# Attention biases that come finished by transfer, and low weight parts from an accumulating transfer

## The chip, the cores and the metric

The kernel runs on one core of a Trainium2 chip. The metric is the device time of one execution in microseconds (us); before the change it is 1277.18 us, the median of 3 runs (1276.97 to 1279.51).

The core's engines are named as the profile names them: PE is TensorE (matrix products), DVE is VectorE, ACT is ScalarE, POOL is GpSimd, and SP is the engine whose queue issues most transfers. Each engine works through its own list of instructions in order, and waits for the others at semaphores. Transfers that SP or GpSimd issue run beside them on the DMA engines.

## The reference

Two residual layers of width 1024 over 512 tokens. The first mixes by a gated unit (gMLP), the second by an attention with a forget gate (FoX), and each is followed by a channel MLP with a squared ReLU. All inputs are 32-bit floats. The change touches the attention alone:

```python
def fox_mixer(h, w_in, b_f, q_g, k_g, w_out):
    p = h @ w_in
    q, k, v, gate, f_logit = jnp.split(p, [W, 2 * W, 3 * W, 4 * W], axis=-1)
    ...
    log_f = jax.nn.log_sigmoid((f_logit + b_f).astype(jnp.float32))
    c = jnp.cumsum(log_f, axis=1).transpose(0, 2, 1)
    for i in range(S // Q_BLOCK):
        ...
        logits = jnp.einsum('bhtd,bhsd->bhts', qb, kb).astype(jnp.float32) * scale
        logits = logits + c[:, :, q0:kend, None] - c[:, :, None, :kend]
        logits = jnp.where(t_idx >= s_idx, logits, -jnp.inf)
        probs = jax.nn.softmax(logits, axis=-1).astype(vb.dtype)
        outs.append(jnp.einsum('bhts,bhsd->bhtd', probs, vb))
    ...
    o = o * jax.nn.sigmoid(gate)
    return o @ w_out
```

There are 16 heads of width 64; `c` is the running sum of the log forget gates, and the bias of a query t on a key s is `c[t] - c[s]`. Rows are worked in 4 blocks of 128 queries, and block i sees the first (i + 1) x 128 keys.

## The kernel before

**Products in three parts.** PE multiplies numbers of a shorter format (fp32r). So each 32-bit factor is cut in a high part, which is its copy in that format, and a low part, which is what the copy lacks; a product is high x high + high x low + low x high (`mm3`, whose matmuls the profile shows at L243). For weights this is done by the class `Stream`. It cuts all weights into chunks of up to 128 x 1024 numbers and for each chunk does three things in order: `_load` (L80) fetches it from HBM into one of 3 buffers `raw` through SP's queue; ACT copies it into the high part `wh` (L85); and another engine subtracts, `wl = raw - wh` (L86). There are 4 buffers each for `wh` and `wl`. `take` hands a chunk to the products and at that moment starts the cut of the third chunk after it, and the load of the third after that.

**Who subtracts.** For most chunks L86 runs on DVE. The 52 chunks of the attention (20 of 768 columns, 16 of 1024, 12 of 512 and 4 of 800) are in the range `ws.pooled`, and there it runs on POOL.

**The attention stage.** It takes the stretch from about 610 to 925 us. The weights of a pair of heads are projected (`project`, matmuls `pq`), and beside them, one matmul group at a time, run the attention steps of the pair before (`attend`): norms of q and k (L722 to L726, of which L725 is a power on POOL and L726 the scaling of `y` on DVE), turns by PE (`tq`, `tk`), logits (`lg`), softmax, turns of the probabilities (`tp`, copied to high and low parts `pth` and `ptl` at L842 and L843), products with the values (`ot`), and the output gate. The gates (`pg`) and the output projection (`po`) are further work between them. The order of PE's instructions in this stage is fixed in the program; a scheduler places the instructions of the other engines and of SP around it.

**The bias.** Once, `forget` works out `c` for all heads: `ct` holds -c with a token per partition, `cs` holds c with a head per row, and SP writes `cs` to a scratch tensor `cd` in HBM (L652). Then, for each head, SP fetches its row of `cd` into all 128 partitions (`cb`, L785, two buffers), and for each block i POOL adds the block's own column of `ct` (L792, tile `bias{i}`, one buffer for each i) and sets the entries of later keys in the diagonal square to a large number (L794). Since the sign of the logits is turned, DVE adds bias and logits and takes the least of each row in one instruction (L803); ACT takes the exponential and its row sums (L804); DVE takes the reciprocal (L806) and scales the four blocks (L808).

**The order around the change.** POOL's list in this stage holds L86, L792, L794, L725 and a few sums of squares of the norms at its ends; DVE's list holds all of the softmax besides the exponential; SP's list holds the loads of the chunks and the fetches of `cb`, and a transfer there that waits for its buffer holds back what is queued behind it.

Of the kernel before, what the change touches and what calls it, by code (L numbers as in the profile page):

```python
# [8 lines left out]
F32 = mybir.dt.float32  # L9
F32R = mybir.dt.float32r  # L10
AF = mybir.ActivationFunctionType
ALU = mybir.AluOpType
# [4 lines left out]
P = 128  # L17
D = 1024
S = 512
KB = D // P  # L20
NT = S // P
E = 2 * D
FF = 4 * D
H = 16
# [30 lines left out]
class Stream:  # L55
# [27 lines left out]

    def _parts(self, hi, lo, t, eng):
        self.nc.scalar.activation(hi, t, AF.Copy)  # L85
        eng.tensor_tensor(lo, t, hi.bitcast(F32), op=ALU.subtract)  # L86

    def _split(self):
        nc, i = self.nc, self.split
        kind = self.chunks[i][1]  # L90
        t, n = self.raw[i] if kind == "first" else self.raw.pop(i)
        hi = self.pool.tile([P, CHUNK_COLS], F32R, tag="wh", name=f"wh{i}", bufs=self.bufs[1])
        lo = self.pool.tile([P, CHUNK_COLS], F32R, tag="wl", name=f"wl{i}", bufs=self.bufs[1])
        eng = nc.gpsimd if i in self.pooled else nc.vector
        pieces = [slice(n // 2, n)] if kind == "second" else self._pieces(i, n)
        for sl in pieces:
            self._parts(hi[:, sl], lo[:, sl], t[:, sl], eng)
        self.parts[i] = (hi, lo)
        if kind == "second":
            self._sums(i, self.raw.pop(i - 1)[0], t)  # L100
        self.split += 1

    def _sums(self, i, f, g):
        nc, sp = self.nc, self.sums_pool
# [9 lines left out]
        for q, s in enumerate((s12, s43)):  # L114
            hi = sp.tile([P, 2, h], F32R, tag="sh", name=f"sh{i}_{q}", bufs=2)
            lo = sp.tile([P, 2, h], F32R, tag="sl", name=f"sl{i}_{q}", bufs=2)
            self._parts(hi, lo, s, nc.vector)
            made += [(hi[:, e], lo[:, e]) for e in range(2)]
# [20 lines left out]
def trunk(ctx: ExitStack, tc: tile.TileContext, A, out, stages=4):  # L139
    nc = tc.nc  # L140
    pe, dve, act, pool = nc.tensor, nc.vector, nc.scalar, nc.gpsimd
# [6 lines left out]
    dram = ctx.enter_context(tc.tile_pool(name="dram", bufs=1, space=DRAM))  # L148
# [15 lines left out]
    chunks = []  # L164
# [21 lines left out]
    chunks += mlp_chunks(A["m0_1"], A["m0_2"])  # L186
    lo_pool = [len(chunks)]
    if stages > 2:
        for kind, n in FOX_ORDER:
# [8 lines left out]
            elif kind == "w":  # L198
                chunks += [A["fw_o"][n, m] for m in range(2)]
    lo_pool.append(len(chunks))  # L200
    if stages > 3:
        chunks += mlp_chunks(A["m1_1"], A["m1_2"])
    ws = Stream(nc, wp, chunks, bufs=(3, 4), ahead=3, load_ahead=3, halved=(0, 1))
    ws.pooled = range(*lo_pool)

# [142 lines left out]
    with ExitStack() as st:  # L348
# [6 lines left out]
        for g in range(4):  # L355
            pv = [(psB if g == 1 and i < 3 else psA)(f"pv{g}_{i}") for i in range(NT)]
            for c in range(4):
                wh, wl = (t.rearrange("p (k n) -> p k n", k=2) for t in ws.take())
                for i in range(NT):
                    for kk in range(2):  # L360
                        k = 2 * c + kk
                        sl = slice(i * P, (i + 1) * P)
# [243 lines left out]
    with ExitStack() as st:  # L606
        fs = st.enter_context(tc.tile_pool(name="fs", bufs=2))
        fp = st.enter_context(tc.tile_pool(name="fp", bufs=2))
# [13 lines left out]
        ct = fp.tile([P, NT, H], F32, tag="ct", name="ct", bufs=1)  # L622
        cd = dram.tile([H, S], F32, tag="cd", name="cd")

        def forget(pq):

            fl = fp.tile([P, NT, H], F32, tag="fl", name="fl", bufs=1)
# [23 lines left out]
            act.activation(cs, pt[:H], AF.Copy, scale=-1.0)  # L651
            nc.sync.dma_start(cd, cs)  # L652
            did.add("F")
# [104 lines left out]
        def attend(p, y):  # L758
# [21 lines left out]
            for e in range(2):  # L780
                hd = 2 * p + e
                yield lag, ("T", p - 1, e) if p else "F"
                lag = 0.0
                cb = fp.tile([P, S], F32, tag="cb", name=f"cb{hd}")
                nc.sync.dma_start(cb, cd[hd].partition_broadcast(P))  # L785
                ees = []
                sm = fs.tile([P, NT], F32, tag="sm", name=f"sm{hd}")
                mn = fs.tile([P, NT], F32, tag="mn", name=f"mn{hd}")
                for i in range(NT):
                    n = (i + 1) * P  # L790
                    bi = fp.tile([P, n], F32, tag=f"bias{i}", name=f"bias{hd}_{i}", bufs=1)
                    pool.tensor_scalar(bi, cb[:, :n], 1.0, ct[:, i, hd : hd + 1], op0=ALU.mult, op1=ALU.add)  # L792
                    dg = bi[:, i * P :]
# [182 lines left out]
```

## Time and profile before

| | us |
|---|---|
| median of 3 runs | 1277.18 |
| the profiled execution | 1277.01 |
| its span in the profile | 1275.3 |

A time is that of a whole execution; the span is the part of it between the first and the last instruction in the profile, here 1.7 us less. The page of the profile gives, for each engine, the busy time, its share of the span and the number of instructions; the number after an x is always a count. A row of a group names the line of the kernel, the engine, the operation, what it writes and reads, the shapes and the count, then the busy time and the mean length of one in ns, and last the idle time of the engine ahead of it and what ended it. A row of waits names who waited, for whom, the sum in us, how often, and the longest. In a table of windows a row begins with its start and end and its length in us; then come the busy times of PE, PEld (the loading of PE's weights), DVE, ACT and POOL with the number of instructions, the granted clock of PE, and the share of time that the DMA engines worked, with GB/s. Busy time of a group is a union, so that neighbours which overlap by some 0.07 us make it a little less than count x mean.

### The profile page before, as it was taken

Reading aid. Unit: us, or ns where it says so; the run is one execution under the profiler, and the core shown is the slowest. Engines: PE = TensorE matmul, PEld = TensorE weight load, DVE = VectorE, ACT = ScalarE, POOL = GpSimd, SP = SyncE. Lnnn points to the kernel's source line nnn. Section 1 sums busy time; section 2 is a strip of 40 time slices with the busy share of each in tenths; the row PEclk is TensorE's granted clock in tenths of the full one; section 3 lists DMA queues with packets and bytes.
Section 4 is the critical chain, followed back from the end, with each engine's and each line's share of the span. In section 5 each row is a group of like instructions: output and inputs, shape, how many; then the busy total and the mean of one; then the engine's idle time right before and its main releaser. Section 6 shows DMA issues by size and latency. Waiting matters only on the chain.

```text
span 1275.3 us, 18354 instructions
## 1 busy us (share of the span) xinstructions
PE 1262.1 (99%) x7108; PEld 1114.0 (87%) x7108; DVE 877.2 (69%) x1206; ACT 624.9 (49%) x981; POOL 484.7 (38%) x415
## 2 busy tenths in 40 slices
PE   9999999999999999999999999999999999999998
PEld 7888888888999999998899899898888999999987
DVE  7347767677867676765537777777887767676763
ACT  7334423246534344443467687678465444444430
POOL 4108433025423232310657667667173322323200
PEclk9999999999999999999999999999999999999999
DMA  7333233233233332323223222223223323232321
GB/s 250 97 107 92 83 91 91 84 98 93 90 116 100 100 102 97 111 89 96 80 81 103 84 82 76 84 77 106 83 67 116 116 84 116 84 116 83 118 81 66
DMA packets 39607, 124.01 MB, mean 97 GB/s; under 512 B 4816, under 2 KB 5840, under 8 KB 39520
## 3 DMA queue, kind: packets, MB, share of 16 engines
q1 hardware_dynamic: 39232, 122.82, 30.4%
q8 instruction: 56, 0.92, 0.3%
q14 instruction: 31, 0.25, 0.1%
q10 hardware_dynamic: 288, 0.02, 0.0%
HBM read 120.69 MB, written 2.13 MB: 96 GB/s over the span
## 4 chain that ended last, share of the span: by engine, by line
PE 89%; DVE 6%; ACT 2%; issue 1%; POOL 1%; DMA 1%; DVEq 0%; ACTq 0%; POOLq 0%
PE po L243 36%; PE da L243 11%; PE bc L243 9%; PE pq L243 8%; PE pv L243 8%; PE pu L243 7%; PE ph L243 3%; PE pg L243 2%; PE ot L243 2%; DVE xl L271 1%; PE lg L243 1%; PE tp L248 1%; PE sp L426 1%; DVE ee L808 1%; DVE y L726 1%
## 5 line engine op out<-in xcount | busy, mean ns | idle before, releaser
L85 ACT ACTIVATE wh<-raw 128x1024 fp32r<-128x1024 f32 (+3 forms) x230 | 219.7, 957 | 270.9 <-PE po L243 83.5
L86 DVE TENSOR_TENSOR wl<-raw,wh 128x1024 fp32r<-128x1024 f32 (+1 forms) x178 | 252.5, 1432 | 46.2 <-ACT wh L85 45.4
L243 PE MATMUL po<-zl,wh 128*128 128x512 f32 x512 | 200.6, 392 | 1.3 <-DVE zl L500 1.3
L243 PE MATMUL po<-zh,wh 128*128 128x512 f32 x512 | 199.9, 391 | 0.0
L243 PE MATMUL po<-zh,wl 128*128 128x512 f32 x512 | 199.5, 390 | 0.0
L556 DVE TENSOR_TENSOR x<-x,po 128x512 f32<-128x512 f32 x128 | 87.2, 683 | 106.1 <-PE po L243 106.1
L86 POOL TENSOR_TENSOR wl<-raw,wh 128x768 fp32r<-128x768 f32 (+3 forms) x52 | 102.4, 1969 | 125.7 <-ACT wh L85 123.2
L110 POOL TENSOR_TENSOR ssum<-raw 128x512 f32<-128x512 f32 x26 | 35.5, 1364 | 268.6 <-DMA raw<-in_m_dram 256.8
L85 ACT ACTIVATE sh<-ssum 128x1024 fp32r<-128x1024 f32 x52 | 55.2, 1061 | 164.5 <-POOL ssum L111 95.8
L243 PEld LDWEIGHTS po<-zh,wl 128*128 128x128 f32 x512 | 96.2, 188 | 19.5
L243 PEld LDWEIGHTS po<-zh,wh 128*128 128x128 f32 x512 | 96.5, 188 | 17.9
L243 PEld LDWEIGHTS po<-zl,wh 128*128 128x128 f32 x512 | 96.6, 189 | 17.8 <-DVE zl L500 1.6
L243 PE MATMUL pq<-wh,xh 128*128 128x384 f32 (+2 forms) x256 | 88.4, 345 | 0.0
L410 POOL TENSOR_SCALAR vn<-v,mv,lnr 128x128 f32<-128x128 f32 x64 | 63.1, 999 | 59.5 <-DVE vl L414 59.4
L243 PE MATMUL pq<-wh,xl 128*128 128x384 f32 (+2 forms) x256 | 83.1, 325 | 0.0
L243 PE MATMUL pq<-wl,xh 128*128 128x384 f32 (+2 forms) x256 | 82.7, 323 | 0.0
L86 DVE TENSOR_TENSOR sl<-ssum,sh 128x1024 fp32r<-128x1024 f32 x52 | 65.9, 1268 | 18.2 <-ACT sh L85 18.1
L112 POOL TENSOR_TENSOR ssum<-raw,ssum 128x512 f32<-128x512 f32 x26 | 37.1, 1428 | 69.1 <-DVE sl L86 68.8
L243 PE MATMUL da<-th,sl 128*128 128x256 f32 x208 | 58.9, 283 | 0.0
L243 PE MATMUL da<-tl,sh 128*128 128x256 f32 x208 | 58.8, 283 | 0.0
L243 PE MATMUL pv<-wh,xh 128*128 128x512 f32 (+1 forms) x160 | 58.0, 372 | 0.7 <-ACT wh L85 0.7
L243 PE MATMUL pv<-wl,xh 128*128 128x512 f32 (+1 forms) x160 | 58.7, 368 | 0.0
(212 smaller groups left out, 3489.9 us busy)
## 6 DMA issues: line engine op xcount, KB each, us to landing
raw<-in_m_dram SPq DMA_DIRECT2D x128, 512.0 KB, 3.6
raw<-in_gw_u_dram SPq DMA_DIRECT2D x16, 512.0 KB, 3.5
raw<-in_gw_o_dram SPq DMA_DIRECT2D x16, 512.0 KB, 3.5
raw<-in_fw_qkv_dram SPq DMA_DIRECT2D x20, 384.0 KB, 3.0
raw<-in_gw_v_dram SPq DMA_DIRECT2D x14, 512.0 KB, 3.9
raw<-in_fw_g_dram SPq DMA_DIRECT2D x8, 512.0 KB, 3.4
cb<-cd SPq DMA_DIRECT2D x16, 256.0 KB, 3.3
raw<-in_fw_o_dram SPq DMA_DIRECT2D x8, 512.0 KB, 3.5
```

Source lines behind the costliest of these rows:

```text
L85: self.nc.scalar.activation(hi, t, AF.Copy)
L86: eng.tensor_tensor(lo, t, hi.bitcast(F32), op=ALU.subtract)
L110: tt(s12[:, 0], a21, a22, op=ALU.add)
L112: tt(s43[:, 0], a12, s12[:, 1], op=ALU.subtract)
L243: ins = pe.matmul(dst, a, b, start=start, stop=stop, skip_group_check=more)
L248: placed(pe.transpose(dst, src, ident[: src.shape[0], : src.shape[0]]), 256)
L271: dve.scalar_tensor_tensor(l, x[b], gcol, h.bitcast(F32), op0=ALU.mult, op1=ALU.subtract)
L410: pool.tensor_scalar(vn[:, i], v[i][:, cb * P : (cb + 1) * P], mv[:, i, 0:1], lnr[:, i : i + 1], op0=ALU.subtract, op1=ALU.mult)
L426: pe.matmul(dst, vh[:, 2 * c + i], wide, start=True, stop=False)
L556: dve.tensor_tensor(x[b], x[b], pt, op=ALU.add)
L726: dve.tensor_tensor(yh, yh, sf.unsqueeze(2).to_broadcast([P, NT * 4, DH]), op=ALU.mult)
L808: dve.tensor_scalar(ees[i], ees[i], rc[:, i : i + 1], None, op0=ALU.mult)
```

## The change

Both parts concern the attention.

The low parts. For the 52 chunks POOL subtracts no more. ACT makes the high part as before; DVE writes its negative into `wl`; and POOL issues a transfer that fetches the chunk from HBM a second time and adds it onto `wl`. So `wl` ends as chunk - high part. The range is called `added`, and the class needs no engine for `_parts` any more.

The biases. `forget` now subtracts for each block i the column c[:, 128 i] from the row (DVE, 16 partitions), and writes four rows for each head to `cd`, now of H x 4 x S. For each head and block one fetch brings the finished differences into `bias{i}`, which has two buffers for i < 3 and one for i = 3; POOL's L792 is gone and its mask stays. What a row of queries lacks to the full bias is the same number for all of its keys, and the softmax takes it out again.

```diff
-    def _parts(self, hi, lo, t, eng):
+    def _parts(self, hi, lo, t):
         self.nc.scalar.activation(hi, t, AF.Copy)
-        eng.tensor_tensor(lo, t, hi.bitcast(F32), op=ALU.subtract)
+        self.nc.vector.tensor_tensor(lo, t, hi.bitcast(F32), op=ALU.subtract)
...
-        eng = nc.gpsimd if i in self.pooled else nc.vector
         pieces = [slice(n // 2, n)] if kind == "second" else self._pieces(i, n)
         for sl in pieces:
-            self._parts(hi[:, sl], lo[:, sl], t[:, sl], eng)
+            if i in self.added:
+
+                nc.scalar.activation(hi[:, sl], t[:, sl], AF.Copy)
+                nc.vector.tensor_scalar(lo[:, sl], hi[:, sl].bitcast(F32), -1.0, None, op0=ALU.mult)
+                nc.gpsimd.dma_start(lo[:, sl], self.chunks[i][0][:, sl], accum_op=ALU.add)
+            else:
+                self._parts(hi[:, sl], lo[:, sl], t[:, sl])
...
-    ws.pooled = range(*lo_pool)
+    ws.added = range(*added)
...
-        cd = dram.tile([H, S], F32, tag="cd", name="cd")
+        cd = dram.tile([H, NT, S], F32, tag="cd", name="cd")
+
+        def bias_tile(i, name):
+            return fp.tile([P, (i + 1) * P], F32, tag=f"bias{i}", name=name, bufs=2 if i < 3 else 1)
...
-            nc.sync.dma_start(cd, cs)
+            for i in range(NT):
+                n = (i + 1) * P
+                shifted = bias_tile(i, f"cs{i}")
+                dve.tensor_scalar(shifted[:H], cs[:, :n], cs[:, i * P : i * P + 1], None, op0=ALU.subtract)
+                nc.sync.dma_start(cd[:, i, :n], shifted[:H])
...
-                cb = fp.tile([P, S], F32, tag="cb", name=f"cb{hd}")
-                nc.sync.dma_start(cb, cd[hd].partition_broadcast(P))
+                bias = []
+                for i in range(NT):
+                    bias.append(bias_tile(i, f"bias{hd}_{i}"))
+                    nc.sync.dma_start(bias[i], cd[hd, i, : (i + 1) * P].partition_broadcast(P))
...
-                    bi = fp.tile([P, n], F32, tag=f"bias{i}", name=f"bias{hd}_{i}", bufs=1)
-                    pool.tensor_scalar(bi, cb[:, :n], 1.0, ct[:, i, hd : hd + 1], op0=ALU.mult, op1=ALU.add)
+                    bi = bias[i]
                     dg = bi[:, i * P :]
                     pool.affine_select(dg, dg, pattern=[[-1, P]], compare_op=ALU.is_ge, fill=BIG, base=0, channel_multiplier=1)
```

PE's list is the same, instruction for instruction. The lists of the others change so, in the softmax of the second pair of heads (heads 2 and 3). On DVE before, where `ee_3_6450` is the last block of head 3, whose bias `bias_3_6442` comes from POOL, and the L808 rows scale head 2:

```order
L803 ISA ee_1_6422,mn_6371<-lg_1_6423,bias_1_6383 128x256
L803 ISA mn_6371 128x1
L806 RECIPROCAL rc_6356<-sm_6283 128x4
L803 ISA ee_2_6436,mn_6371<-lg_2_6437,bias_2_6428 128x384
L803 ISA mn_6371 128x1
L808 TENSOR_SCALAR ee_0_6293<-ee_0_6293,rc_6356 128x128
L808 TENSOR_SCALAR ee_1_6316<-ee_1_6316,rc_6356 128x256
L808 TENSOR_SCALAR ee_2_6333<-ee_2_6333,rc_6356 128x384
L808 TENSOR_SCALAR ee_3_6350<-ee_3_6350,rc_6356 128x512
L723 TENSOR_REDUCE yss_6402<-ysq_1_6406 128x8
L803 ISA ee_3_6450,mn_6371<-lg_3_6451,bias_3_6442 128x512
```

And now (L817 is the old L803, L820 the old L806, L822 the old L808, L736 the old L723):

```order
L817 ISA ee_1_6447,mn_6399<-lg_1_6448,bias_1_6392 128x256
L817 ISA mn_6399 128x1
L99 TENSOR_SCALAR wl_6440<-wh_6439 128x768
L820 RECIPROCAL rc_6378<-sm_6312 128x4
L817 ISA ee_2_6459,mn_6399<-lg_2_6460,bias_2_6394 128x384
L817 ISA mn_6399 128x1
L822 TENSOR_SCALAR ee_0_6320<-ee_0_6320,rc_6378 128x128
L822 TENSOR_SCALAR ee_1_6342<-ee_1_6342,rc_6378 128x256
L822 TENSOR_SCALAR ee_2_6357<-ee_2_6357,rc_6378 128x384
L822 TENSOR_SCALAR ee_3_6372<-ee_3_6372,rc_6378 128x512
L736 TENSOR_REDUCE yss_6426<-ysq_1_6430 128x8
L817 ISA ee_3_6471,mn_6399<-lg_3_6472,bias_3_6396 128x512
```

The negation of one chunk (L99) has come in ahead of the reciprocal of head 2; the rest stands as it did. On POOL at the same place before (`bias_3_6442` is the last block of head 3, `bias_0_6664` to `bias_2_6695` the first ones of head 4):

```order
L792 TENSOR_SCALAR bias_1_6383<-cb_6368,ct 128x256
L794 AFFINE_SELECT bias_1_6383<-bias_1_6383 128x128
L792 TENSOR_SCALAR bias_2_6428<-cb_6368,ct 128x384
L794 AFFINE_SELECT bias_2_6428<-bias_2_6428 128x128
L792 TENSOR_SCALAR bias_3_6442<-cb_6368,ct 128x512
L792 TENSOR_SCALAR bias_0_6664<-cb_6660,ct 128x128
L794 AFFINE_SELECT bias_3_6442<-bias_3_6442 128x128
L794 AFFINE_SELECT bias_0_6664<-bias_0_6664 128x128
L86 TENSOR_TENSOR wl_6416<-raw_6163,wh_6415 128x768
L792 TENSOR_SCALAR bias_1_6678<-cb_6660,ct 128x256
```

And now (L808 is here the old L794, the mask; `bias_3_6396` is the last block of head 3, `bias_0_6684` to `bias_2_6688` are of head 4):

```order
L100 DMA wl_6332<-in_fw_qkv_dram 128x768
L808 AFFINE_SELECT bias_0_6684<-bias_0_6684 128x128
L808 AFFINE_SELECT bias_1_6686<-bias_1_6686 128x128
L808 AFFINE_SELECT bias_2_6688<-bias_2_6688 128x128
L808 AFFINE_SELECT bias_3_6396<-bias_3_6396 128x128
L100 DMA wl_6440<-in_fw_qkv_dram 128x768
L808 AFFINE_SELECT bias_0_6770<-bias_0_6770 128x128
L808 AFFINE_SELECT bias_1_6772<-bias_1_6772 128x128
```

POOL's additions are gone, a transfer's issue (L100) stands where a subtraction stood, and the masks of three blocks of head 4 now come ahead of that of the last block of head 3. On SP before, fetches of `cb` (`cb_6281` is that of head 2, `cb_6368` of head 3) between loads of weights:

```order
L785 DMA cb_6281<-cd 128x512
L80 DMA raw_5867<-in_fw_qkv_dram 128x768
L80 DMA raw_5917<-in_fw_g_dram 128x1024
L785 DMA cb_6368<-cd 128x512
L80 DMA raw_6001<-in_fw_qkv_dram 128x768
L785 DMA cb_6660<-cd 128x512
```

And now (`bias_0_6304` to `bias_3_6310` are of head 2, `bias_3_6005` of head 1, `bias_0_6390` to `bias_2_6394` of head 3):

```order
L800 DMA bias_0_6304<-cd 128x128
L80 DMA raw_5941<-in_fw_g_dram 128x1024
L800 DMA bias_1_6306<-cd 128x256
L800 DMA bias_2_6308<-cd 128x384
L800 DMA bias_3_6005<-cd 128x512
L800 DMA bias_0_6390<-cd 128x128
L80 DMA raw_6024<-in_fw_qkv_dram 128x768
L800 DMA bias_1_6392<-cd 128x256
L800 DMA bias_2_6394<-cd 128x384
L800 DMA bias_3_6310<-cd 128x512
```

Four fetches stand for one, the last block of a head is fetched after the first blocks of the next head, and weights are queued between them.

More of the change, by code (lines that the diff above doesn't have):

```diff
@@ L116, in _sums @@
             lo = sp.tile([P, 2, h], F32R, tag="sl", name=f"sl{i}_{q}", bufs=2)
-            self._parts(hi, lo, s, nc.vector)
+            self._parts(hi, lo, s)
             made += [(hi[:, e], lo[:, e]) for e in range(2)]
@@ L186, in trunk @@
     chunks += mlp_chunks(A["m0_1"], A["m0_2"])
-    lo_pool = [len(chunks)]
+    added = [len(chunks)]
     if stages > 2:
@@ L199, in trunk @@
                 chunks += [A["fw_o"][n, m] for m in range(2)]
-    lo_pool.append(len(chunks))
+    added.append(len(chunks))
     if stages > 3:
```

## The prediction

> **What bounds the kernel now.** I read the page's first rows, then one table of windows over the attention stage, then the waits of TensorE, then the two engines that release it. The page first (busy us and share of the span of each engine; then the chain that ended last):
>
> ```profile
> span 1275.3 us, 18354 instructions
> PE 1262.1 (99%) x7108; PEld 1114.0 (87%) x7108; DVE 877.2 (69%) x1206; ACT 624.9 (49%) x981; POOL 484.7 (38%) x415
> PE 89%; DVE 6%; ACT 2%; issue 1%; POOL 1%; DMA 1%; DVEq 0%; ACTq 0%; POOLq 0%
> ```
>
> TensorE is idle for 1275.3 - 1262.1 = 13.2 us in all. Neither VectorE nor GpSimd is full, so nothing that the change takes off them is worth time by itself: it is worth only what it shortens of TensorE's idle time, and only in the stage that it touches. Windows over that stage (start:end, length, busy PE, PEld, DVE, ACT, POOL, then the clock, DMA share and GB/s):
>
> ```profile
> 660.00:670.00 10.00, 9.29 (x58) 8.97 (x57) 6.31 (x8) 5.87 (x10) 5.42 (x9) 1.00 0.35 108
> 680.00:690.00 10.00, 9.58 (x61) 8.75 (x61) 8.01 (x17) 6.59 (x16) 8.83 (x7) 1.00 0.30 100
> 710.00:716.00 6.00, 4.13 (x28) 3.57 (x27) 5.17 (x14) 4.76 (x9) 4.85 (x5) 1.00 0.30 84
> 716.00:720.00 4.00, 3.29 (x22) 2.91 (x21) 3.76 (x6) 1.75 (x4) 0.80 (x1) 1.00 0.35 98
> 860.00:870.00 10.00, 9.44 (x60) 7.88 (x58) 8.58 (x21) 7.31 (x20) 8.37 (x11) 1.00 0.44 132
> 870.00:880.00 10.00, 9.74 (x80) 9.39 (x78) 7.41 (x14) 8.82 (x14) 4.28 (x3) 1.00 0.17 55
> 880.00:925.00 45.00, 44.37 (x233) 36.91 (x232) 36.56 (x75) 26.37 (x53) 16.98 (x15) 1.00 0.29 94
> sum 275.00, PE 269.36 PEld 244.53 DVE 203.74 ACT 200.15 POOL 168.73; mean PE 20.72 PEld 18.81 DVE 15.67 ACT 15.40 POOL 12.98
> ```
>
> The last row is for all of 650 to 925: TensorE idles 275.0 - 269.4 = **5.6 us**, and the rows above hold 0.71, 0.42, 1.87, 0.71, 0.56, 0.26 and 0.63 of it. That is the ceiling of the gain, 0.44% of the kernel. The waits of TensorE there (us in total, times, longest):
>
> ```profile
> PE tp L248 <- DVE ptl L843: 3.6, 4, 1.9
> PE tq L248 <- DVE y L726: 1.0, 2, 0.7
> PE ot L243 <- DVE v L677: 0.6, 1, 0.6
> ```
>
> All are ended by VectorE, none by GpSimd and none by a transfer. So the change must help through VectorE, or not at all. The longest wait, near 713, on VectorE (start, us, instruction):
>
> ```profile
> 704.04 0.68 DVE L803 CUSTOM_DVE_ANT_0 ee<-lg,bias 128x512 f32<-128x512 f32 x1
> 707.13 2.74 DVE L808 TENSOR_SCALAR ee<-ee,rc 128x128 f32<-128x128 f32 x4
> 710.38 0.68 DVE L803 CUSTOM_DVE_ANT_0 ee<-lg,bias 128x512 f32<-128x512 f32 x1
> 712.16 1.27 DVE L808 TENSOR_SCALAR ee<-ee,rc 128x128 f32<-128x128 f32 x4
> 715.35 2.53 DVE L726 TENSOR_TENSOR y<-y,yss 128x1024 f32<-128x1024 f32 x1
> ```
>
> and on GpSimd at that time:
>
> ```profile
> 706.33 1.85 POOL L86 TENSOR_TENSOR wl<-raw,wh 128x768 fp32r<-128x768 f32 x1
> 708.15 1.07 POOL L792 TENSOR_SCALAR bias<-cb,ct 128x256 f32<-128x256 f32 x2
> 709.19 0.83 POOL L794 TENSOR_SCALAR_AFFINE_SELECT bias<-bias 128x128 f32<-128x128 f32 x2
> ```
>
> The same four L808 take 2.74 us beside GpSimd's L86 and L792, and 1.27 us five us later. VectorE is slowed by what runs on GpSimd, and the softmax behind it, and then TensorE, are late.
>
> **What the change removes.** GpSimd's two groups, and what the two VectorE groups cost in the mean, beside clean ones:
>
> ```profile
> L86 POOL TENSOR_TENSOR wl<-raw,wh 128x768 fp32r<-128x768 f32 (+3 forms) x52 | 102.4, 1969 | 125.7 <-ACT wh L85 123.2 <-issue 2.5
> L792 POOL TENSOR_SCALAR bias<-cb,ct 128x128 f32<-128x128 f32 (+1 forms) x64 | 38.4, 606 | 18.1 <-DVE mn L803 12.3 <-DVE kl L775 4.6 <-DVE yss L724 1.2
> L808 DVE TENSOR_SCALAR ee<-ee,rc 128x128 f32<-128x128 f32 (+1 forms) x64 | 28.6, 508 | 0.4
> L726 DVE TENSOR_TENSOR y<-y,yss x8: 1215/1652/3424, 660.0 to 871.9; 128x1024 f32<-128x1024 f32 x8
> L726 DVE TENSOR_TENSOR y<-y,yss 128x1024 f32<-128x1024 f32 x8 | 15.8, 1972 | 3.7 <-POOL yss L725 3.7
> L808 DVE TENSOR_SCALAR ee<-ee,rc 128x512 f32<-128x512 f32 x1 | 0.5, 481 | 0.0
> L808 DVE TENSOR_SCALAR ee<-ee,rc 128x384 f32<-128x384 f32 x1 | 0.4, 415 | 0.0
> L808 DVE TENSOR_SCALAR ee<-ee,rc 128x256 f32<-128x256 f32 x1 | 0.3, 348 | 0.0
> L808 DVE TENSOR_SCALAR ee<-ee,rc 128x128 f32<-128x128 f32 x1 | 0.3, 287 | 0.0
> ```
>
> GpSimd loses 102.4 + 38.4 = 140.8 us. L808 has 64 x 0.508 = 32.5 us of durations; sixteen clean runs of 0.481 + 0.415 + 0.348 + 0.287 = 1.53 make 24.5, so 8.0 us are contention. L726 has 15.8 against 8 x 1.215 = 9.7 (the least of its three figures), so 6.1 more. VectorE is relieved of about **14 us**.
>
> **What it adds to VectorE.** One negation for each of the 52 chunks (20 of 768 columns, 16 of 1024, 12 of 512, 4 of 800). The trace has no such instruction; L808 is nearest: same operation, one SBUF source, f32. From its clean rows (481 - 287) / 384 = 0.505 ns a column on 287 at 128 columns, so 0.48, 0.61, 0.63 and 0.74 us, together 12.2 + 11.8 + 5.8 + 2.5 = **32 us**. The low bound is this price; the high one is L726's clean 1.215 for 1024 columns, 1.19 ns a column, 49 us for the 41,088 columns. I take 32. VectorE goes from 203.7 to about 222 us in 275, 81%. It is covered where VectorE waits for ACT or TensorE anyway (71 us idle in this stage), and not covered inside the softmax run of a pair of heads. The four 16-row subtractions cost about 0.29 to 0.48 each, 1.5 us once, while VectorE waits for the first qs.
>
> **What it adds to the queues.** Plain transfers land so (KB each, median us from issue):
>
> ```profile
> raw<-in_fw_g_dram SPq DMA_DIRECT2D x8, 512.0 KB, 3.4
> cb<-cd SPq DMA_DIRECT2D x16, 256.0 KB, 3.3
> ```
>
> The last bias block of a head has one buffer: it can be fetched only after the previous head's L803 has read it. In the run above that read ends at 704.72; 3.3 to land and 0.29 to 0.4 for the mask (the two L794 above take 0.83) give about 708.5, ahead of the 710.38 at which the reader now starts. Almost two us are spare, so it costs nothing here. All weight loads share SP's queue with these fetches, and a fetch that waits for its buffer holds the loads behind it. What the two wait for now:
>
> ```profile
> SPq L80 <- POOL wl L86: 188.7, 39, 7.1
> DVE ee L803 <- POOL bias L794: 1.5, 2, 1.0
> ```
>
> The loads wait for GpSimd's subtraction to free a buffer; in the changed kernel ACT's copy frees it, some 2 us sooner, so I put no cost on a load behind a fetch. Traffic: 41,088 columns x 512 B = 21 MB of weights a second time, and 16 x 1280 x 512 B = 10.5 MB of biases for 4.2, against a share of 0.17 to 0.44 now: less than twice, no bound.
>
> The accumulating transfer itself is not in the trace, nor its issue on GpSimd. Its issue lies between nothing and the 1.97 us mean of the L86 that it replaces, its landing between the 3.4 us of a plain load and, with no row to limit it, three times that, 10.2. I take 1.2 and 5. What it may take is shown by the chunk with the least time between ACT's high part and its first use of the low part:
>
> ```profile
> 850.84 1.06 ACT L85 ACTIVATE wh<-raw 128x1024 fp32r<-128x1024 f32 x1
> 863.05 0.39 PE L243 MATMUL pg<-xh,wl 128*128 128x512 f32 x1
> ```
>
> 863.05 - 851.90 = 11.1 us. Negation 0.74, up to 2 us in VectorE's and GpSimd's queues, 1.2 and 5 make 8.9: hidden, with 2 us to spare. [...]
>
> **The sum, by place.** At 660 to 670 TensorE waits for y:
>
> ```profile
> 660.00 2.85 DVE L726 TENSOR_TENSOR y<-y,yss 128x1024 f32<-128x1024 f32 x1 [1.72 <-POOL yss L725]
> ```
>
> At 1.22 it ends 1.6 us sooner: the 0.71 goes. At 710 to 716 the L808 run ends at 708.4 instead of 709.9; a negation now stands just ahead of it (0.61), and L803 moves from 710.38 to about 709.7: 0.7 of the 1.87 goes. At 716 to 720 y falls from 2.53 to 1.22: the 0.71 goes. At 870 to 880 another y: 0.26 goes. At 680 to 690 the L808 were clean, so nothing. At 860 to 870 and 880 to 925 L808 gains about what an added negation costs. Sum: 0.71 + 0.7 + 0.71 + 0.26 = **2.4 us**. The profiled execution took 1277.01 us, 1.7 more than its span; the median of the runs is 1277.18, so the two bases differ by 0.2. 1277.18 - 2.4 = **1274.8**.
>
> **Rivals.** (a) *More than that.* If contention is all that makes VectorE late, all 5.6 us go: about 1272. For it: every wait is ended by VectorE. Against: 32 us are put on it for 14 taken off. (b) *Nothing.* The order on VectorE, not its pace, sets the waits; gains and negations cancel: 1277. For it: at 680 to 690 the L808 were clean and TensorE waited all the same. (c) *VectorE becomes the bound, slower.* Negations stand inside the softmax run of every pair. If the relief does not come, because GpSimd's issue of a transfer slows VectorE as its subtraction did, two negations of 0.6 fall in the run of each of the five pairs that show a wait: 5 x 1.2 = 6 us, 1283. It decides once a negation costs more than the 1.2 to 1.5 us that a contended run of L808 loses now. [...] (d) *The accumulating transfer is late, slower.* From a landing of 7 us the tightest chunks run out of cover; at 10.2 the one above is 3.2 us late, and two or three like it make about 7: 1284. For it: no row of the trace bounds it from above. Against: a plain load takes 3.4.
>
> **How the numbers follow.** The measurement tells a change of about 0.2%, 2.55 us, from none. Chances: forecast 0.50 (its own range 1272.8 to 1276.5, half of it beyond 0.2%), (a) 0.15, (b) 0.11, (c) 0.13, (d) 0.11. Faster 0.25 + 0.15 = 0.40; same 0.25 + 0.11 = 0.36; slower 0.24. The range reaches from just under (a) to (c) and (d): 1271 to 1284.
>
> **What would show it.** In the changed profile: the means of L808 and L726 (L822 and L739 there) near 400 ns and 1.2 us, L99 near 0.6 us and 32 us in all, TensorE's idle time in 650 to 925 at about 3.2 us, no wait of TensorE ended by a DMA into wl or bias. It is wrong if L808 stays near 508 ns, if waits of TensorE name wl, or if L803 waits for bias for more than the 1.5 us in all of the row above.

## The result, and the profile after

The changed kernel takes **1293.31 us** in the median of 3 runs (1290.08 to 1295.5) against 1277.18: a ratio of 1.0121, with a 95% interval of 1.0095 to 1.0147. It is slower by 16 us, outside the range of 1271 to 1284. The page of the changed kernel (span, busy time of the engines, the chain by engine, and the two DMA queues with packets, MB and share of 16 engines):

```profile
span 1293.8 us, 18505 instructions
...
PE 1269.0 (98%) x7108; PEld 1120.8 (87%) x7108; DVE 884.0 (68%) x1262; ACT 625.1 (48%) x981; POOL 393.3 (30%) x351
...
q1 hardware_dynamic: 46240, 129.17, 31.3%
q0 software_dynamic: 7488, 21.04, 10.1%
...
PE 86%; DVE 5%; DMA 4%; ACT 2%; POOL 2%; issue 2%; SPq 0%; POOLq 0%; DVEq 0%; ACTq 0%
```

The profiled execution is the slowest of the three (1295.5 us), so the profile shows more than 16 us: the span grew by 1293.8 - 1275.3 = 18.5 us. TensorE's idle time went from 13.2 to 1293.8 - 1269.0 = 24.8 us, which is 11.6 of it; and its busy time went from 1262.1 to 1269.0 with the same 7108 matmuls, which is the other 6.9. The second part is new: the same work ran slower. In the chain, transfers now hold 4% (1% before).

Windows of the changed kernel, the first four from among those that the prediction read, then four around two new stalls, then the stage (the last three columns are the granted clock, the DMA share and GB/s):

```profile
660.00:670.00 10.00, 10.00 (x64) 9.97 (x63) 6.95 (x16) 7.24 (x11) 1.55 (x6) 1.00 0.64 145
680.00:690.00 10.00, 9.19 (x60) 8.57 (x59) 7.66 (x18) 4.85 (x12) 5.51 (x6) 1.00 0.93 223
710.00:716.00 6.00, 4.36 (x28) 3.40 (x27) 5.83 (x13) 4.71 (x11) 5.47 (x5) 1.00 0.69 171
716.00:720.00 4.00, 4.00 (x25) 3.84 (x24) 1.92 (x5) 2.15 (x4) 0.00 (x0) 1.00 0.63 108
745.00:750.00 5.00, 2.83 (x20) 2.44 (x19) 3.90 (x7) 3.21 (x6) 3.62 (x4) 0.98 0.57 150
750.00:755.00 5.00, 5.00 (x23) 4.77 (x22) 0.95 (x4) 1.35 (x3) 0.00 (x0) 0.68 0.51 82
780.00:785.00 5.00, 1.93 (x11) 1.61 (x10) 2.44 (x4) 0.61 (x2) 4.68 (x4) 0.89 0.54 97
785.00:790.00 5.00, 5.00 (x24) 4.72 (x24) 1.60 (x4) 2.20 (x4) 0.00 (x0) 0.77 0.65 105
...
650.00:925.00 275.00, 256.88 (x1523) 234.82 (x1521) 196.21 (x481) 190.81 (x405) 85.22 (x116) 0.97 0.72 167
```

and the last of these windows in the kernel before:

```profile
650.00:925.00 275.00, 269.36 (x1611) 244.53 (x1610) 203.74 (x456) 200.15 (x419) 168.73 (x182) 1.00 0.28 87
```

Up to 720 the change did most of what was forecast: the 0.71 us at 660 to 670 and the 0.71 at 716 to 720 are gone, 710 to 716 lost 0.23 of its 1.87; 680 to 690, for which nothing was forecast, grew by 0.39. The loss lies where TensorE had hardly waited before: 2.17 us in 745 to 750 (0.24 before), 3.07 in 780 to 785 (none before). After each the granted clock is down, 0.68 and 0.77. And the DMA engines are busy for 0.72 of the stage instead of 0.28. Waits of the changed kernel (us in total, times, longest):

```profile
POOL bias L808 <- DMA bias<-cd: 67.3, 35, 7.2
...
PE tp L253 <- DVE ptl L857: 13.0, 10, 3.1
DVE ee L817 <- POOL bias L808: 11.5, 9, 3.0
...
DVE y L739 <- POOL yss L738: 8.7, 5, 3.9
...
PE po L248 <- DVE v L690: 3.7, 1, 3.7
```

TensorE still names VectorE alone, and no wait names `wl`. But VectorE waits for GpSimd, for the mask of a bias 11.5 us (1.5 before) and for the power 8.7 (3.7 before), and GpSimd waits 67.3 us for the fetches of biases. Transfers in the changed kernel (KB each, median us to landing):

```profile
raw<-in_fw_qkv_dram SPq DMA_DIRECT2D x20, 384.0 KB, 4.5
wl<-in_fw_qkv_dram POOLq DMA_DIRECT2D x20, 384.0 KB, 6.2
...
wl<-in_fw_g_dram POOLq DMA_DIRECT2D x8, 512.0 KB, 7.1
bias<-cd SPq DMA_DIRECT2D x16, 256.0 KB, 4.9
...
bias<-cd SPq DMA_DIRECT2D x16, 64.0 KB, 4.6
```

A fetch of 256 KB lands in 4.9 us instead of 3.3, and one of 64 KB hardly sooner.

**Two places show how this reaches TensorE.** First, VectorE of the changed kernel near 900 (start, us, instruction, and in brackets what it waited for):

```profile
893.91 0.68 DVE L817 CUSTOM_DVE_ANT_0 ee<-lg,bias 128x512 f32<-128x512 f32 x1
...
899.34 0.61 DVE L690 SCALAR_TENSOR_TENSOR v<-pv,rstd,v 128x128 fp32r<-128x128 f32 x2
902.92 0.69 DVE L817 CUSTOM_DVE_ANT_0 ee<-lg,bias 128x512 f32<-128x512 f32 x1 [2.98 <-POOL bias L808]
...
903.54 0.86 DVE L690 SCALAR_TENSOR_TENSOR v<-pv,rstd,v 128x128 fp32r<-128x128 f32 x3
```

The last block of one head is read until 894.59. Only then can its one buffer be fetched again; the next head's block is there 8.3 us later, of which the fetch takes 7.8. VectorE waits 2.98 us, and behind it in VectorE's list stand the copies of the values (L690) that TensorE waits 3.7 us for. Second, GpSimd near 780:

```profile
774.57 0.29 POOL L808 TENSOR_SCALAR_AFFINE_SELECT bias<-bias 128x128 f32<-128x128 f32 x1 [2.56 <-DMA bias<-cd]
775.77 0.29 POOL L808 TENSOR_SCALAR_AFFINE_SELECT bias<-bias 128x128 f32<-128x128 f32 x1 [0.90 <-DVE mn L817]
777.47 0.32 POOL L808 TENSOR_SCALAR_AFFINE_SELECT bias<-bias 128x128 f32<-128x128 f32 x1 [1.41 <-DMA bias<-cd]
778.00 1.35 POOL L100 DMA_DIRECT2D wl<-in_fw_qkv_dram  x1 [0.21 <-PE tp L253]
778.59 3.72 POOL L738 TENSOR_TENSOR yss<-yss,mhalf 128x16 f32<-128x16 f32 x1
```

and VectorE there:

```profile
774.97 0.69 DVE L817 CUSTOM_DVE_ANT_0 ee<-lg,bias 128x512 f32<-128x512 f32 x1 [1.54 <-POOL bias L808]
...
776.30 0.17 DVE L737 SCALAR_TENSOR_TENSOR yss<-yss,epsr 128x16 f32<-128x16 f32 x1
...
782.35 1.31 DVE L739 TENSOR_TENSOR y<-y,yss 128x1024 f32<-128x1024 f32 x1 [2.61 <-POOL yss L738]
783.58 1.21 DVE L857 TENSOR_TENSOR ptl<-tp,pth 128x256 fp32r<-128x256 f32 x3
```

The input of the power (L737) is ready at 776.47, but GpSimd stands at a mask whose fetch has not landed, then issues a transfer, and begins the power at 778.59. It takes 3.72 us; `y` waits for it, and `ptl`, for which TensorE is waiting, is queued behind `y`. In the kernel before that power began at 774.15:

```profile
774.15 2.91 POOL L725 TENSOR_TENSOR yss<-yss,mhalf 128x16 f32<-128x16 f32 x1
```

So there are two waits: **A**, the minimum (L817) waits for a block whose fetch could start late; **B**, the power waits in GpSimd's list behind masks that wait for fetches.

### The profile page after: what moved, and what is told of

Its sections match the earlier page's. It is cut to its first block, busy times and chain, and to the rows that moved or that the text cites. A ratio compares the mean times of both kernels' runs of the same rounds, so it can differ in the third digit from the quotient of the medians.

```text
span 1293.8 us, 18505 instructions
## 1 busy us (share of the span) xinstructions
PE 1269.0 (98%) x7108; PEld 1120.8 (87%) x7108; DVE 884.0 (68%) x1262; ACT 625.1 (48%) x981; POOL 393.3 (30%) x351
## 3 DMA queue, kind: packets, MB, share of 16 engines
q1 hardware_dynamic: 46240, 129.17, 31.3%
q0 software_dynamic: 7488, 21.04, 10.1%
## 4 chain that ended last, share of the span: by engine, by line
PE 86%; DVE 5%; DMA 4%; ACT 2%; POOL 2%; issue 2%; SPq 0%; POOLq 0%; DVEq 0%; ACTq 0%
PE po L248 37%; PE da L248 11%; PE bc L248 8%; PE pv L248 7%; PE pu L248 7%; PE pq L248 7%; DMA bias<-cd 3%; PE ph L248 3%; PE ot L248 1%; PE pg L248 1%; PE tp L253 1%; POOL yss L738 1%; PE sp L431 1%; PE lg L248 1%; DVE xl L276 1%
## 5 line engine op out<-in xcount | busy, mean ns | idle before, releaser
L85 ACT ACTIVATE wh<-raw 128x1024 fp32r<-128x1024 f32 (+1 forms) x178 | 174.9, 984 | 245.6 <-PE po L248 78.9
L86 DVE TENSOR_TENSOR sl<-ssum,sh 128x1024 fp32r<-128x1024 f32 x52 | 64.8, 1247 | 18.2 <-ACT sh L85 18.1
L98 ACT ACTIVATE wh<-raw 128x768 fp32r<-128x768 f32 (+3 forms) x52 | 44.9, 863 | 29.2 <-PE pq L248 14.5
L248 PE MATMUL da<-th,sh 128*128 128x256 f32 x208 | 58.6, 282 | 0.0
```

What stands on the lines that cost most here:

```text
L86: self.nc.vector.tensor_tensor(lo, t, hi.bitcast(F32), op=ALU.subtract)
L98: nc.scalar.activation(hi[:, sl], t[:, sl], AF.Copy)
L248: ins = pe.matmul(dst, a, b, start=start, stop=stop, skip_group_check=more)
```

## The experiments

Ratios are to the kernel before on the same chip, with 95% intervals; the median of before was 1276.8 to 1277.2 in these comparisons.

### The parts one by one

The first run is the changed kernel with this in place of negation and transfer:

```diff
-                nc.vector.tensor_scalar(lo[:, sl], hi[:, sl].bitcast(F32), -1.0, None, op0=ALU.mult)
-                nc.gpsimd.dma_start(lo[:, sl], self.chunks[i][0][:, sl], accum_op=ALU.add)
+                nc.gpsimd.tensor_tensor(lo[:, sl], t[:, sl], hi[:, sl].bitcast(F32), op=ALU.subtract)
```

> The biases by transfer as in the changed kernel; the low parts by GpSimd's subtraction as before. Theory T1 (a fetch for each head and block, the last of them into a single buffer, comes too late by itself): well over half of the loss stays, 1286 to 1290 us, the 512-column block still waits about 3.5 us or more for its fetch, and TensorE still has stalls of over 2 us. Rival R1 (the second traffic of the accumulating transfers makes every fetch slow): fetches land in about 3 us again as in the kernel before, and the time is within 3 us of 1277. Rival R2 (the negations overload VectorE): 1275 to 1277, since they are gone here.

The second has the changed `_split` in the kernel before, with `cb`, L792 and L794 as they were:

> The low parts by negation and accumulating transfer as in the changed kernel; the biases fetched once a head and added by GpSimd as before. T1: within 2 us of 1277. R1: the one fetch a head lands in about 5 us instead of 3.3 but has two buffers, so 1277 to 1281. R2: most of the loss, 1286 or more, with waits of TensorE ended by VectorE and no waits for a fetch.

The third is the first with `nc.vector` for `nc.gpsimd`, the fourth the kernel before with that subtraction on VectorE:

> The biases by transfer as in the changed kernel; the low parts by a subtraction on VectorE (1.2 us for 1024 columns, by the row of other chunks 1.43) in place of negation and transfer: VectorE carries more than in the changed kernel, the DMA system less. T1: 1286 or more, as without it. R1: 1277 to 1282. R2: 1295 or more, since VectorE has twice the added load.

> The kernel before with the low parts by a subtraction on VectorE instead of GpSimd: no transfer is added anywhere. This measures VectorE's load alone. T1 and R1: within 4 us of 1277. R2: 1290 or more.

| | low parts by GpSimd's subtraction | by VectorE's subtraction | by accumulating transfer |
|---|---|---|---|
| `cb`, added on GpSimd | 1277.2 (before) | 1277.67, 1.0006 (0.9996 to 1.0015) | 1276.64, 0.9996 (0.9987 to 1.0005) |
| biases by transfer | 1285.77, 1.0079 (1.0064 to 1.0094) | 1277.66, 1.0009 (1.0000 to 1.0018) | 1293.31, 1.0121 (1.0095 to 1.0147) |

R2 is out: VectorE carries the negations, or the whole subtraction, and costs nothing. T1 is out as it stood: the same four fetches into the same buffers cost at most 0.2% where VectorE subtracts. R1 fails by the first run, and is right for the third. The second and fourth come out within 0.7 us of the kernel before, close to what T1 and R1 both had forecast. How long GpSimd waits is no sign of the loss: in the third run it waits 153.6 us for the fetches, and nothing that TensorE needs is late for it. Neither half of the change is harmful by itself in every setting; the biases are, beside one of two things. The second traffic is the one to settle for the changed kernel.

### Traffic or the order of GpSimd

Both runs are the changed kernel with another way to the low part. The fifth run adds 128 columns of each chunk by transfer and subtracts the rest on VectorE; the sixth subtracts all on VectorE and writes the low part to a scratch tensor that nothing reads:

```diff
+                k = P
                 nc.scalar.activation(hi[:, sl], t[:, sl], AF.Copy)
-                nc.vector.tensor_scalar(lo[:, sl], hi[:, sl].bitcast(F32), -1.0, None, op0=ALU.mult)
-                nc.gpsimd.dma_start(lo[:, sl], self.chunks[i][0][:, sl], accum_op=ALU.add)
+                nc.vector.tensor_scalar(lo[:, :k], hi[:, :k].bitcast(F32), -1.0, None, op0=ALU.mult)
+                nc.gpsimd.dma_start(lo[:, :k], self.chunks[i][0][:, :k], accum_op=ALU.add)
+                nc.vector.tensor_tensor(lo[:, k:n], t[:, k:n], hi[:, k:n].bitcast(F32), op=ALU.subtract)
```

> The changed kernel, but only the first 128 columns of each of the 52 chunks get their low part by negation and accumulating transfer; the rest is subtracted on VectorE. GpSimd issues as many transfers, each behind a wait for VectorE, with a tenth of the bytes. Theory TQ (GpSimd's list in order: issues that wait for VectorE stand among the masks and the power, and delay them): 1285 us or more. Theory TT (traffic: the bytes of the second fetch make the biases land late): the share of the DMA engines in 650 to 925 falls from 0.72 to about 0.4, fetches of biases land in about 3.6 us, and the time is at most 1280.

```diff
-                nc.vector.tensor_scalar(lo[:, sl], hi[:, sl].bitcast(F32), -1.0, None, op0=ALU.mult)
-                nc.gpsimd.dma_start(lo[:, sl], self.chunks[i][0][:, sl], accum_op=ALU.add)
+                nc.vector.tensor_tensor(lo[:, sl], t[:, sl], hi[:, sl].bitcast(F32), op=ALU.subtract)
+                spare = self.spare.tile([P, CHUNK_COLS], F32, tag=f"spare{i}", name=f"spare{i}")
+                nc.gpsimd.dma_start(spare[:, :n], lo[:, sl].bitcast(F32))
```

> The low parts by a subtraction on VectorE, and for each of the 52 chunks GpSimd issues a plain transfer that writes the low part to a scratch tensor in HBM which nothing reads. GpSimd's list is that of the run with 128 columns but for the size of the transfers: issues, waits for VectorE and full bytes, and TensorE waits for none of these transfers. TT: slower than the run with 128 columns by 5 us or more if the share of the DMA engines rises to 0.6 or more. TQ: within 2 us of the run with 128 columns.

The stage with 128 columns, then with the writes, and last, from the page of the run with the writes, the queue of GpSimd's transfers:

```profile
650.00:925.00 275.00, 266.66 (x1602) 242.68 (x1601) 225.60 (x546) 198.39 (x415) 85.54 (x117) 1.00 0.46 121
```

```profile
650.00:925.00 275.00, 265.64 (x1594) 241.21 (x1593) 223.50 (x500) 196.50 (x414) 69.62 (x117) 1.00 0.55 174
```

```profile
q0 software_dynamic: 5184, 21.04, 4.0%
```

With 128 columns: 1278.2 us, 1.0008 (0.9999 to 1.0017); with the writes 1282.13, 1.0035 (1.0024 to 1.0046). As many issues with as many waits for VectorE cost nothing measurable, so TQ as it stood (issues that delay the masks) is out. More bytes with the same list of GpSimd (and 52 instructions less on VectorE) cost 3.9 us, more than the 2 of TQ. The share reached 0.55, short of the 0.6 that TT's figure was for, and the loss is short of its 5. At four shares of the stage, 0.36 (third run), 0.46, 0.55 and 0.72 (the changed kernel), a fetch of 256 KB lands in 3.6, 3.7, 4.2 and 4.9 us, and the time is 1277.7, 1278.2, 1282.1 and 1293.3. The second traffic is needed for this loss, and without the four fetches it costs nothing (1276.64 at a share of 0.68). Between 0.55 and 0.72 more than the traffic differs (who makes the low part, and that TensorE needs what the transfers bring), so the runs do not show that this last step is traffic alone.

### What the late fetches hold up

To take wait B away, the masks leave GpSimd. VectorE adds a tile of 0 and 2^100 to the logits:

```diff
...
-                    pool.affine_select(dg, dg, pattern=[[-1, P]], compare_op=ALU.is_ge, fill=BIG, base=0, channel_multiplier=1)
...
+                    at_ = lg[:, i * P : n]
+                    dve.tensor_tensor(at_, at_, late, op=ALU.add)
```

> The changed kernel with the masks off GpSimd: VectorE adds a tile of 0 and 2^100 to the diagonal square of the logits in PSUM, 64 instructions of about 0.3 us, so that nothing on GpSimd waits for a fetch of biases; VectorE's minimum waits for it by itself. TQ: y waits for the power at most 3.7 us in all as before, and the time falls to 1278 to 1284. TT: the 512-column blocks still come 5 to 8 us after their buffer is free, VectorE waits for the fetches directly, and the time stays at 1287 or more.

The eighth run is the same edit in the first run's kernel:

> As the run with the masks on VectorE, but with the low parts by GpSimd's subtraction as before, without the second traffic. TQ: with no mask on GpSimd no subtraction stands behind a fetch, and no fetch behind a load that waits for a subtraction: 1277 to 1280 instead of 1285.8. TT has no traffic to name here; if fetches are late in themselves, because the 512-column block has one buffer, 1284 or more.

To take wait A away, all blocks have two buffers (`bufs=2`), in the changed kernel and in the first run's:

> The changed kernel with two buffers for the last block too (room is made by laying four small tiles of the forget gate into a block's tile): every fetch can start while the block of the head before is still to be read. Theory TJ (the fetch of the last block starts only when its one buffer has been read, 5 to 8 us land in the path with the second traffic, and the masks, the issues and the power that are queued behind it on GpSimd come late): 1276 to 1282, waits of VectorE for the mask under 3 us, no stall of TensorE over 2.2 us. Rival TF (four fetches a head in SP's one list behind loads are late whatever the buffers): 1287 or more.

> The same two buffers in the kernel with the biases by transfer alone and GpSimd's subtraction (1285.8 with one buffer). TJ: 1276 to 1280. TF: 1284 or more.

And in one run each head has one fetch into two buffers. The masks are with VectorE there too, and `cd` holds one row a head again (both left out here):

```diff
-                bias = []
-                for i in range(NT):
-                    bias.append(bias_tile(i, f"bias{hd}_{i}"))
-                    nc.sync.dma_start(bias[i], cd[hd, i, : (i + 1) * P].partition_broadcast(P))
+                cb = fp.tile([P, S], F32, tag="cb", name=f"cb{hd}")
+                nc.sync.dma_start(cb, cd[hd].partition_broadcast(P))
...
-                    bi = bias[i]
+                    bi = cb[:, :n]
```

> The changed kernel's low parts with all of their traffic, but one fetch of the unshifted row a head into two buffers, no addition of the query's own term (the softmax takes it out), and the mask added to the logits by VectorE; nothing on GpSimd but the issues and the power. TJ: 1276 to 1280, since a fetch has a head's time to land. TF: the same. A theory that the second traffic alone or VectorE's load makes TensorE wait: 1284 or more.

Waits of VectorE in the stage with the masks on VectorE, and with two buffers:

```profile
DVE ee L821 <- DMA bias<-cd: 7.3, 6, 1.7
DVE y L743 <- POOL yss L742: 2.1, 2, 1.3
```

```profile
DVE y L738 <- POOL yss L737: 12.4, 7, 4.5
...
DVE ee L816 <- POOL bias L807: 0.6, 2, 0.3
```

Each edit removed one wait and left the other: without masks on GpSimd `y` waits 2.1 us for the power (8.7 in the changed kernel) while the minimum still waits 7.3 for fetches; with two buffers the minimum waits 0.6 (11.5) and `y` 12.4. The times are 1285.21, 1.0061 (1.0045 to 1.0078), and 1288.41, 1.0088 (1.0070 to 1.0106). TJ promised that two buffers do it all, and fails; TQ that the masks do, and fails by 1 us; TT, 1287 or more with the masks on VectorE, fails by 2. TF's 1287 or more with two buffers comes true here. One fetch a head: 1279.53, 1.0019 (1.0010 to 1.0029), as TJ and TF had it, so the second traffic with VectorE's load is not the loss. Nor is it the work of the masks on GpSimd (26.0 us in the changed kernel): with 128 columns the masks and as many issues stand in its list, `y` waits 2.3 us for the power, and the time is 1278.2.

The next run has both edits, with four fetches a head and all of the traffic:

> The changed kernel with both mends: masks added to the logits by VectorE, so that no power on GpSimd stands behind a fetch, and two buffers for the last block. Each alone left 1285.2 and 1288.4. Theory TB (two waits in the place of one: the minimum for the last block's fetch, through its one buffer, and the power for masks that wait for fetches of later heads; the second traffic makes both long): both go, 1277 to 1281 with four fetches a head and all of the traffic, waits of y for the power under 3 us, waits of VectorE for a fetch under 2 us. Rival TF (four fetches a head in SP's list behind loads are late whatever is done): 1284 or more, while one fetch a head gave 1279.5.

```profile
DVE y L744 <- POOL yss L743: 1.8, 2, 1.3
...
DVE ee L822 <- DMA bias<-cd: 0.5, 1, 0.5
```

It takes 1280.52 us, 1.0031 (1.0019 to 1.0043), with fetches of 256 KB that still land in 5.1 us. Both waits are gone, 12.8 of the 16 us with them, and TF is out for the changed kernel: four late fetches do no harm when nothing that TensorE needs stands behind them. The 3.5 us that stay have the 64 additions of the masks on VectorE beside them; one fetch a head with the same additions is 1 us faster.

### The other loss, without the second traffic

The kernels with GpSimd's subtraction went another way: 1285.77 as first run, 1286.5, 1.0071 (1.0056 to 1.0086), with masks on VectorE, 1285.95, 1.0070 (1.0043 to 1.0097), with two buffers. TQ and TJ, 1280 at most, fail in these two. The 1284 or more of their rivals comes true; whether by late fetches is the question of two more runs, both edits together, and then one fetch a head:

> The same two mends with GpSimd's subtraction and without the second traffic, where each mend alone left 1286 (and neither 1285.8). TB: the fetches cost nothing any more, and what stays over 1277 is the 18.5 us of additions on a VectorE that GpSimd's subtractions slow: 1278 to 1283. Rival TV (VectorE, slowed by GpSimd's subtractions, is the whole of the loss in the kernel without the second traffic, and fetches none of it): 1285 or more.

> One fetch a head into two buffers, the mask added to the logits by VectorE, no addition of the query's own term, and GpSimd's subtraction as before: no second traffic and no late fetch, but the 18.5 us of additions. TV (on the side of GpSimd's subtraction the additions are what costs in the last run, 1287.8, and fetches nothing): 1285 or more. Rival (the four fetches a head still cost there): 1277 to 1281, as with the second traffic (1279.5).

They take 1287.75, 1.0082 (1.0065 to 1.0099), and 1287.01, 1.0079 (1.0062 to 1.0096). TB, 1283 at most, fails. With no late fetch left the time is the same, as TV's figures had it: in these two the fetches cost nothing measurable, and the additions beside GpSimd's subtractions cost what the fetches had. Groups of VectorE in the last of them:

```profile
L810 DVE TENSOR_TENSOR lg<-lg,late 128x128 f32<-128x128 f32 x64 | 18.6, 294 | 4.5 <-PE lg L247 3.9
...
L735 DVE TENSOR_TENSOR y<-y,yss 128x1024 f32<-128x1024 f32 x8 | 14.8, 1845 | 1.9 <-POOL yss L734 1.9
```

The 18.6 us of additions come with 9.9 us of time; without the subtractions, with one fetch a head, the accumulating transfers and the same additions, the kernel is 2.7 over the one before. TV's reason, a slowed VectorE, is in part argued. The additions take 18.6 us in both kernels, and `y` is scaled in 1.85 us here, 1.97 in the kernel before and 1.22 without the subtractions, so VectorE is not slowed more than it was. What differs is where the slowing falls: in the eighth run, with the same additions beside the same subtractions, the scaling of a head's four blocks takes 2.74 us at 712.81, in the chain that ended last (1.27 in the kernel before, at 712.16), and TensorE waits up to 2.6 us for `ptl` (1.9 before). How much of the 9.9 us comes about in this way was not measured.

That edit cannot tell, then, what makes the first run slow. The first and the third run show that GpSimd's subtractions and the four fetches are both needed for it. In its trace `y` waits 10.3 us for the power (8.7 in the changed kernel), and 11.0 with two buffers, in a profile of that kernel's fastest execution (1281.95 us). Whether the subtractions do it by standing between masks that wait and the power, or by slowing VectorE, was not shown by an experiment; it stays open.

### A version that might pay

In the second run's kernel (biases as before, low parts by transfer) ACT writes the negative from the raw chunk:

```diff
-                nc.vector.tensor_scalar(lo[:, sl], hi[:, sl].bitcast(F32), -1.0, None, op0=ALU.mult)
+                nc.scalar.activation(lo[:, sl], t[:, sl], AF.Copy, scale=-1.0)
```

> A version that might beat both: the low parts by the accumulating transfer alone (1276.6, no different from before) with the negation made by ACT from the raw chunk, so that VectorE loses its 30 us of it and is relieved of GpSimd's contention as well. If VectorE's load sets what is left of TensorE's waits: 1272 to 1275. If its order does, or if ACT with 45 us more of copies in its list ahead of the softmax is late instead: 1276 to 1282.

It takes 1290.13 us, 1.0105 (1.0090 to 1.0120): worse than both forecasts. VectorE's busy time in the stage falls from 216.2 to 180.5 us and buys nothing; ACT's rises from 200.4 to 221.3. VectorE's waits for ACT's `pth` rise from 5.2 to 10.6 us, and for `oz` from 8.4 to 19.7, so that ACT's copies come late is the likeliest reason; no run was made to show it. No version beat the kernel before.

## Why the prediction was wrong

**What held.** The relief of VectorE, almost to the digit. Groups of the changed kernel:

```profile
L99 DVE TENSOR_SCALAR wl<-wh 128x768 fp32r<-128x768 f32 (+3 forms) x52 | 30.3, 582 | 22.4 <-ACT wh L98 22.0
L822 DVE TENSOR_SCALAR ee<-ee,rc 128x128 f32<-128x128 f32 (+1 forms) x64 | 21.5, 398 | 0.4
L739 DVE TENSOR_TENSOR y<-y,yss 128x1024 f32<-128x1024 f32 x8 | 10.1, 1268 | 8.8 <-POOL yss L738 8.7
```

Forecast were 32 us for L99, 400 ns and 1.2 us for the other two. GpSimd's issues did not slow VectorE as its subtractions had (398 ns against 508 for the scalings, 1268 against 1972 for `y`), so rival (c) is out, by these rows and by the 1276.64 us of the transfers alone. Rival (d) is out too, although its landing time came true: 6.2 and 7.1 us against the 5 that was taken, and still no wait for `wl`. With the biases left as they were the transfers' half changed nothing measurable: rival (b), for that half.

**The step that failed first: "Almost two us are spare, so it costs nothing here."** The term that was mis-sized is the landing of the last block's fetch, taken at the 3.3 us of `cb`. VectorE of the changed kernel at that place, first the read that frees the buffer, then the one that waits:

```profile
702.16 0.68 DVE L817 CUSTOM_DVE_ANT_0 ee<-lg,bias 128x512 f32<-128x512 f32 x1
...
708.55 0.69 DVE L817 CUSTOM_DVE_ANT_0 ee<-lg,bias 128x512 f32<-128x512 f32 x1 [1.02 <-POOL bias L808]
```

That it starts at 708.55, where 708.5 was worked out, is luck. The buffer was free at 702.84 instead of 704.72; with 3.3 us and the mask the block would have been there at about 706.5, ahead of the 707.53 at which VectorE could have begun. The fetch took 5.2 us, and VectorE waited 1.02. Near 900 it is the same: free at 894.59, the reader could have begun at 899.95, with 3.3 us the block would have been there at about 898.3, and the fetch took 7.8. The spacing of the heads was not the fault: in the kernel before, the eight places of this kind leave 4.3 to 7.6 us between the end of one read and the start of the next, more than 3.3 + 0.4 in each. And in the third run, with the same fetches into the same buffers but a landing of 3.6 us, VectorE waits only 0.5 us for masks. Wait A is this term. The prediction had named it as a sign of being wrong, at more than 1.5 us: it is 11.5. TensorE's idle time in 650 to 925, expected at 3.2 us, is 275.0 - 256.9 = 18.1.

**The second: "less than twice, no bound" for the traffic.** Bytes a second went from 87 to 167, about as worked out, but the share of the DMA engines from 0.28 to 0.72, 2.6 times. Here a byte that was added took more of them than one that was loaded: in the page of the changed kernel q1 takes 31.3% for 129.17 MB, 0.24% a MB, and q0 10.1% for 21.04 MB, 0.48%, twice that. The prediction priced the landing of the transfer itself, where the error was harmless (5 us taken, 7.1 measured for 512 KB), and not what the transfer does to the others. So the 3.3 us of `cb` was carried over to fetches that take 4.9 in the median.

**The third is a step that is not there.** What the masks wait for was costed at VectorE, which reads them, but not at GpSimd, which makes them in order. The rows of GpSimd's list showed masks of a later head ahead of the rest; that the power of `y` stands behind them was not read. That is wait B, and the removal of both waits brings back 12.8 us.

**The clock added to its size.** No case had TensorE run slower; 6.9 of the 18.5 us in the profile are that, at a granted clock of 0.97 in the stage (1.00 before). The other 11.6, idle time, are by themselves more than the 7 us of the slowest rival.

The ceiling of 5.6 us is sound as a sum, and at the three places up to 720 us whose gain was forecast TensorE did wait less. A ceiling on the gain says nothing of the loss: the price had to be looked for where TensorE did not wait.

## What to carry to other kernels

When an engine that held data at hand (one row for a head, two buffers) is replaced by transfers that arrive just in time, list for each in-order engine what stands behind the instruction that will now wait, in every round of the loop and not only where the profile shows a wait today. Cost added traffic by the share of the DMA engines that it takes, not by its bytes (here 2.6 times the share for 1.9 times the GB/s), and price the longer landing (here 4.9 us for 3.3) at every transfer beside it that something waits for. Two harmless halves can be harmful together: time each alone and both, before a cause is named.

## What the runs showed of the hardware

**Three stalls cost TensorE a second time, by its clock.** In the changed kernel the 5 us after the stalls at 745 and 780 us ran at 0.68 and 0.77 of the clock; the largest stall is followed by half:

```profile
900.00:905.00 5.00, 1.29 (x5) 0.89 (x5) 2.08 (x7) 3.20 (x10) 1.17 (x2) 0.84 1.05 304
905.00:910.00 5.00, 5.00 (x16) 4.02 (x16) 3.53 (x11) 0.59 (x1) 0.86 (x1) 0.50 0.97 175
```

The 1.87 us idle at 710 to 716 in the kernel before, and 1.64 in the changed one, were followed by a clock of 1.00. At 745, 2.17 us of idle time in a stretch of 5 were followed by 0.68, while 2.45 us in 715 to 720 of the first run were followed by 1.00, so idle time in such a stretch does not by itself tell the clock that follows. Busy DMA engines alone did not lower it: with the accumulating transfers alone the stage has a share of 0.68 at a clock of 1.00.

**In these kernels an added byte took 2.0 times the time of a loaded one on the DMA engines, and 2.5 times that of one written to HBM** (0.48% against 0.24% of the span for a MB in the changed kernel; 10.1% in it against 4.0% in the sixth run for the same 21.04 MB from the same queue).

**A small fetch landed hardly sooner than a large one** beside other traffic: 64 KB in 4.6 us, 256 KB in 4.9 (3.1 and 3.4 without the second traffic, in the first run's kernel with two buffers), so four fetches a head were four landings to wait for.
